# Attention output turned feature-major by 32x32 block transposes on VectorE and by its trip through HBM, in place of 64 transposes on TensorE

## The chip, the cores and the metric

The kernel runs on one core of one Trainium2 chip. The metric is the device time of that core in microseconds (us). Three runs of the kernel before gave 1374.78, 1375.06 and 1375.9 us; the median, 1375.06 us, is the time before.

## The reference

One layer of a hybrid encoder block, in float32, on x of 1024 tokens by 1024 features. Cut to what matters here:

```python
h = rmsnorm(x, norm_mix)
q, k, v, r, lr_f, lr_b, u, g_a, g_b = split(h @ w_in)
# gated linear attention, 4 heads (keys 128 wide, values 256 wide), forward and backward
o = gla(q, k, v, decay_fwd) + flip(gla(flip q, flip k, flip v, decay_bwd))
o = o * rsqrt(mean(o * o, axis=-1) + EPS)        # per head and token
o = o.reshape(tokens, 1024) * gla_norm           # one gain per feature
o = o * silu(r)                                  # the output gate
y_a = o @ w_branch_gla
...
merged = sigmoid(g_a) * y_a + sigmoid(g_b) * y_b # y_b: the pooling branch, from u
x = x + merged @ w_out
...                                              # feed-forward layer, last norm
```

The place of the change is between `o` and `y_a`: the four heads' normalized outputs are multiplied by the gain and by silu(r), and become an operand of the product with `w_branch_gla`.

## The kernel before

**Numbers.** Every large product runs as three products on TensorE: each f32 operand is split in a high part (a cast on ScalarE) and a low part (a subtraction on VectorE or GpSimd), and `products` (line 273) adds high x high, high x low and low x high into one PSUM bank. `mm3` (line 275) is such a triple, 512 columns wide as a rule, and calls `pump` behind it.

**Order of the work.** The program's order is written out by hand, and each engine runs its instructions in that order. A generator for the attention of a head yields after each part, with the cost of the part in units of one 512-wide triple. `pump` counts the triples down and lets the next thing into the program when its time has come: first what `soon(delay, ...)` put off, then a split of weights that were loaded, then the jobs that run beside, then the next part of the attention. So attention's small steps lie between the triples of the projections.

**Memory.** SBUF holds 39 slots of 128 x 1024 f32, given out in turn; four buffers for raw weights, six each for their high and low parts; five small temporaries (`t2`). PSUM has three banks for the large products and five for all else (`ps_g`).

**Loads and writes.** All of them are issued on SyncE's queue, in program order: an issue that waits holds up all issues behind it. Weights are loaded by `load` (line 208) one step ahead of use, cast to the high part on ScalarE (line 200), and the low part is made on GpSimd (line 201). Writes to HBM are not issued where the data is made: `later` notes them, and `flush` (line 563) issues all that are noted.

**The attention of head h** (`attention`, from line 813) makes the decays, the keys, the chunk states and scores, and at its end, for each of eight token tiles, 128 tokens x 256 values of output, copied to one of two slots `o[half]` of 4 x 256 per partition (line 999). Tokens lie on the partitions, features along the row. `rms_scale` (line 1012) makes the norm's factors. `normalize` (line 1016) scales the eight tiles with one VectorE instruction each (line 1019). For heads 0 to 2 it then notes two writes to `o_out[h]`; it is called from the next head's attention, and the writes are issued some 3.5 units later. For head 3 it is called where the attention ends, and head 3's output stays in SBUF. That end falls inside the last triple of half 0 of column tile j = 3 of the loop below.

**The r loop** (lines 1212 to 1242) projects six of r's eight column tiles, j = 0 to 5, 128 features each. The result is feature-major: features on the partitions, tokens along the row, 512 of them in each of two halves. Each turn:

- at j = 2, 3 and 4 reads back the output of head 0, 1 and 2 (`load_o`, line 1033; tiles `ol`);
- takes the weights of j and issues the load and the splits of the next (`take`);
- at j = 4 loads the weights of the gate unit 0 (`fraw`, line 1085), which are the last two column tiles of r;
- for each half runs eight triples (`feature_major`), and after half 0 calls `flush` (line 1231);
- for j < 3 keeps r in SBUF (the attention isn't done yet); from j = 3 on gates one of the kept tiles and its own.

From j = 3 on, `feature_parts` (line 669) also runs beside: it reads eight sums of h back from HBM (`hs`, line 673), which ScalarE casts (`trh`, line 707) and VectorE subtracts from (`trl`, line 698), for products in Strassen's manner (seven products for eight blocks, from sums of blocks). The gate units' weights are combined in the same manner (`fs`, line 1093).

**The gate** (`gated`, line 1182) takes one feature tile of 128 and one half of 512 tokens: Silu of r on ScalarE (`sr`, line 1185); four transposes of 128 x 128 on TensorE into one PSUM bank `tp` (line 1188), since the attention's output is token-major and r is feature-major; then one VectorE instruction that multiplies the bank by the gain and by `sr` (line 1195). When a pair of tiles is whole for both halves, two writes of the gated output are noted and flushed 2 units later. The last two feature tiles are gated after the loop, when gate unit 0 is done. Eight tiles by two halves by four transposes are the 64 transposes.

Of the kernel before, what the change touches and what calls it, by code (L numbers as in the profile page):

```python
# [10 lines left out]
F32 = mybir.dt.float32  # L11
# [4 lines left out]
ALU = mybir.AluOpType  # L16

P = 128
# [3 lines left out]
NT = SEQ // P  # L22
HALF = 512
HEADS = 4
DK = 128
DV = 256
RANK = 16
CH = 128
SUB = 64
GROUPS = 4  # L30
WINDOWS = (2, 4, 8, 16)
PAD = 8
# [21 lines left out]
def kernel(  # L54
# [20 lines left out]
    nc = tc.nc  # L75
# [10 lines left out]
    ps_g = ctx.enter_context(tc.tile_pool(name="ps_g", bufs=8 - MM_BANKS, space=bass.MemoryType.PSUM))  # L86

    dram = ctx.enter_context(tc.tile_pool(name="dram", bufs=1, space=bass.MemoryType.DRAM))
# [4 lines left out]
    def name(s):  # L93
        count[0] += 1
        return f"{s}_{count[0]}"

    def slot(dtype=F32, shape=(2, HALF), s="slot"):
        return slots.tile([P, *shape], dtype, tag="slot", name=name(s))

    def t2(width=HALF, dtype=F32, s="t"):  # L100
        return tmp.tile([P, width], dtype, tag="t2", name=name(s), padded_shape=[P, HALF + 2 * PAD])
# [4 lines left out]
    def vec(width, s="v"):  # L106
        return small.tile([P, width], F32, tag="vec", name=name(s), bufs=12)

    def bank(pool, s="ps"):
        return pool.tile([P, HALF], F32, tag=pool.name, name=name(s))  # L110
# [5 lines left out]
    ident = const.tile([P, P], F32, tag="ident", name="ident")  # L116
# [8 lines left out]
    keep = const.tile([P, 4, P], U8, tag="keep", name="keep")  # L125
    carry = const.tile([P, HALF // SUB, SUB], BF16, tag="carry", name="carry")

# [5 lines left out]

    edge = const.tile([P, 2, GROUPS, PAD], F32, tag="edge", name="edge")
    nc.gpsimd.memset(edge[:, :, :, :], 1.0)
# [18 lines left out]
    def soon(delay, *steps):  # L154
        put_off.extend([delay, step] for step in steps)
# [146 lines left out]
    def rms_scale(ms, width, s):  # L302
        rs = vec(width, s)
        nc.vector.tensor_scalar(rs[:, :], ms, EPS, None, op0=ALU.add)
        nc.gpsimd.tensor_tensor(rs[:, :], rs[:, :], half_neg[:, :width], op=ALU.pow)
        return rs
# [132 lines left out]
    g_mix, g_ffn, g_gla, g_pool = (cols[:, 8 * i : 8 * i + 8] for i in range(4))  # L439
# [118 lines left out]
    def later(dst, src):  # L558
        deferred.append((dst, src))
# [174 lines left out]
    o_heads, unscaled = {}, []  # L734
# [78 lines left out]
    def attention(h):  # L813
# [28 lines left out]
        def decay(half, d):  # L842
# [3 lines left out]
            tot = vec(8, "tot")  # L846
            cs3 = cs.rearrange("p (n c) -> p n c", c=SUB)
            la3 = la.rearrange("p (n c) -> p n c", c=SUB)
            cy = carry.rearrange("p n c -> p (n c)")
            if d == 0:  # L850
                nc.vector.tensor_tensor_scan(cs[:, :], cy, la[:, :], 0.0, op0=ALU.mult, op1=ALU.add)
                nc.vector.tensor_copy(tot[:, :], cs3[:, :, SUB - 1])
            else:
# [4 lines left out]
                )  # L858
                nc.vector.tensor_tensor(tot[:, :], cs3[:, :, SUB - 1], la3[:, :, SUB - 1], op=ALU.add)
            first = cs.rearrange("p (n a c) -> p n a c", a=2, c=SUB)[:, :, 0, :]  # L860
            tot2 = tot.rearrange("p (n a) -> p n a", a=2)
# [62 lines left out]
        def scores(half):  # L924
            sc = [bank(ps_g, "sc") for _ in range(2)]
            for d in range(2):
                for i in range(4):
                    n = 4 * half + i
                    nc.tensor.matmul(
                        sc[d][:, i * CH : (i + 1) * CH], chunk_of(ke, n, d), chunk_of(qe, n, d),  # L930
                        start=True, stop=True,
                    )
            hi, lo = (t2(dtype=F32R, s="p")[:, :] for _ in range(2))
            nc.vector.copy_predicated(sc[1][:, :], keep.rearrange("p n c -> p (n c)"), sc[0][:, :])
            split_to(hi, lo, sc[1][:, :])
            return hi, lo
# [8 lines left out]
        q, k = qk_heads[h]  # L945
# [21 lines left out]
        for n in range(NT - 1, 0, -1):  # L967
            m = n - 1
# [9 lines left out]
        p = scores(0)  # L978
# [3 lines left out]
        o = [slot(shape=(4, DV), s="o") for _ in range(2)]  # L982
        ms = vec(NT, "oms")
        old = sf = None
        for n in range(NT):
            half, i = n // 4, n % 4
# [22 lines left out]
            if n == 3:  # L1009
                p = q_next  # L1010
            yield 1.02
        rs = rms_scale(ms[:, :], NT, "ors")
        if h == HEADS - 1:
            o_heads[h] = o

        def normalize():
            for n in range(NT):
                t = o[n // 4][:, n % 4, :]
                nc.vector.tensor_scalar(t, t, rs[:, n : n + 1], None, op0=ALU.mult)
            if h < HEADS - 1:  # L1020
                for half in range(2):
                    later(o_out[h][:, 4 * half : 4 * half + 4, :], o[half][:, :, :])

        unscaled.append(normalize)
        if h == HEADS - 1:
            unscaled.pop()()

    o_out = [dram.tile([P, NT, DV], F32, name=f"o_out{h}") for h in range(HEADS - 1)]

    def load_o(h):  # L1030
        o_heads[h] = [slot(shape=(4, DV), s="ol") for _ in range(2)]
        for half in range(2):
            nc.sync.dma_start(o_heads[h][half][:, :, :], o_out[h][:, 4 * half : 4 * half + 4, :])

    def sums_behind():
        prepare_beside(map(feature_sums, range(2)), 2)
# [21 lines left out]
    for h in range(HEADS):  # L1058
        if h:
            project_qk(h, h == 2)  # L1060
        else:
            first_qk()
            begin(attention(0))
        if h < HEADS - 1:
            begin(attention(h + 1))
        if h == 0:
            for ts in ((7,), (6,), (5, 4)):
                pair_products(ts)
            prepare_beside(map(branch_jobs, range(4)), 4.2)
        if h == 2:  # L1070
            value_weights.pop().products()
# [110 lines left out]
    def gated(j, half, src):  # L1182

        sr = t2(s="sr")
        nc.scalar.activation(sr[:, :], src, AF.Silu)
        tp = bank(ps_g, "tp")
        for i in range(4):
            nc.tensor.transpose(
                tp[:, i * P : (i + 1) * P],
                o_heads[j // 2][half][:, i, (j % 2) * P : (j % 2 + 1) * P], ident[:, :],  # L1190
            )
        if j // 2 not in oT:
            oT[j // 2] = [slot(s="o") for _ in range(2)], []
        tiles, there = oT[j // 2]
        nc.vector.scalar_tensor_tensor(
            tiles[half][:, j % 2, :], tp[:, :], g_gla[:, j : j + 1], sr[:, :], op0=ALU.mult, op1=ALU.mult
        )
        there.append((j, half))
        if len(there) == 4:
            c = j // 2 % 2  # L1200
            for half, t in enumerate(tiles):
                later(ob_out[j // 4, half][:, 2 * c : 2 * c + 2, :], t[:, :, :])
            soon(2, flush)

    def put_by():

        if raw_r:
            gated(*raw_r.pop(0))
# [3 lines left out]
    for j in range(KT - 2):  # L1212
        if 2 <= j <= 4:
            load_o(j - 2)
# [8 lines left out]
        for half in range(2):  # L1223
            if j >= BY and not sums_begun and (j > BY or not side):
                finish_side()
                finish_beside()
                prepare_beside([feature_parts()], 5)
                sums_begun = True
            ps = feature_major(w, hT, half)
            if half == 0:  # L1230
                flush()
            elif j == KT - 3:
                for _ in range(2):
                    gunits[1].load()
            if j < BY:
                nc.scalar.copy(whole_r[:, half, :], ps[:, :])
                raw_r.append((j, half, whole_r[:, half, :]))
            else:
                put_by()
                gated(j, half, ps[:, :])  # L1240
            if j == KT - 3 and half == 0:
                gates_ahead.step()
# [155 lines left out]

    p_out = dram.tile([GROUPS, 2, P, 2, HALF], F32, name="p_out")
    u_rows = [dram.tile([P, SEQ], F32, name=f"u_rows{g}") for g in range(GROUPS)]  # L1400

# [28 lines left out]
    def pooling():  # L1430

        for g in range(GROUPS):
            u = [t2(HALF + 2 * PAD, s="u") for _ in range(2)]
# [630 lines left out]
    for at, p in enumerate(OUT_ORDER):  # L2064
# [9 lines left out]
        for i in range(CLOSE if closing else n_of):  # L2074
            n = at * n_of + i
# [57 lines left out]
```

## Time and profile before

| what | value |
|---|---|
| median of three runs | 1375.06 us (1374.78 to 1375.9) |
| the profiled execution: span from its first to its last instruction | 1373.4 us |
| TensorE, matmuls | 1361.4 us busy, 99% |
| VectorE | 836.8 us, 61% |
| GpSimd | 752.1 us, 55% |
| ScalarE | 647.3 us, 47% |
| mean granted TensorE clock | 0.999 |
| read and written in HBM | 168.74 MB and 82.05 MB, 183 GB/s over the span |

The profile is of one execution. Times in it are microseconds, or nanoseconds where a row gives a mean for one instruction. PE is TensorE's matmuls and transposes, PEld its loading of weights (which runs beside the matmuls), DVE is VectorE, ACT ScalarE, POOL GpSimd, SP SyncE, which issues the transfers. `L1188` is line 1188 of the kernel. A row such as `o<-tp,cols,sr` names the tile that is written and the tiles that are read, without their numbers. A timeline row begins with the time from the span's start and the duration. A row of waits names an engine, the tile that the waiting instruction writes, and behind the arrow the instruction that released it, with the longest waits in us. Matmuls are pipelined: one of 512 columns lasts 0.39 us from its start to its end, and the next starts before it has ended.

In time, the four attentions lie before some 330 us, the gate's products run from 324.5 to 383.0 us, the last Silu of the r loop is at 353.6 us, and the branches, the merge and the feed-forward layer fill the rest.

### The profile page before, as it was taken

How to read it: one execution, taken by the hardware profiler on the slowest of the kernel's cores; microseconds unless marked ns; L12 is line 12 of the kernel's file. 1: busy time of each engine (PE TensorE's matmuls, PEld its weight loads, DVE VectorE, ACT ScalarE, POOL GpSimd, SP SyncE). 2: the span in 40 equal slices, each digit the busy share in tenths (PEclk: the TensorE clock that was granted, in tenths of full speed). 3: DMA queues.
4: the chain of work that ended last, by engine and by line, in shares of the span. 5: the costliest groups of instructions: out<-in, count | busy, mean ns of one | idle time of the engine just before them, and what ended most of it. 6: DMA issues, size and time to landing. Idle time of an engine off the chain costs nothing. (4 is left out here: it accounts for less than half of the span.)

```text
span 1373.4 us, 17879 instructions
## 1 busy us (share of the span) xinstructions
PE 1361.4 (99%) x6310; PEld 1132.9 (82%) x6310; DVE 836.8 (61%) x1034; ACT 647.3 (47%) x1177; POOL 752.1 (55%) x557
## 2 busy tenths in 40 slices
PE   9999999999999999999999999999999999999998
PEld 7888888888888888888888888888888888888886
DVE  6974556554735777678883955655566556343375
ACT  7365666755534445554346533333333334444253
POOL 3323723222597547667764376666676667455454
PEclk9999999999999999999999999999999999999999
DMA  6321523314778569995416355555544447985451
GB/s 227 113 87 52 181 90 92 95 60 123 245 236 278 186 198 308 373 386 216 150 71 241 112 174 176 176 176 177 176 145 137 146 136 266 384 301 187 169 215 77
DMA packets 167834, 251.97 MB, mean 183 GB/s; under 512 B 11160, under 2 KB 94144, under 8 KB 167744
## 3 DMA queue, kind: packets, MB, share of 16 engines
q1 hardware_dynamic: 167600, 250.57, 53.8%
q8 instruction: 49, 0.80, 0.2%
q14 instruction: 41, 0.34, 0.1%
q10 hardware_dynamic: 144, 0.26, 0.0%
HBM read 168.74 MB, written 82.05 MB: 183 GB/s over the span
## 5 line engine op out<-in xcount | busy, mean ns | idle before, releaser
L201 POOL TENSOR_TENSOR wl<-fs,wh 128x512 fp32r<-128x512 f32 x124 | 173.1, 1400 | 163.5 <-ACT wh L200 104.0
L273 PE MATMUL ps<-gh,wh 128*128 128x512 f32 x616 | 240.5, 390 | 0.0
L273 PE MATMUL ps<-gl,wh 128*128 128x512 f32 x616 | 239.8, 389 | 0.3 <-DVE gl L1691 0.3
L273 PE MATMUL ps<-gh,wl 128*128 128x512 f32 x616 | 239.7, 389 | 0.0
L201 POOL TENSOR_TENSOR wl<-fraw,wh 128x512 fp32r<-128x512 f32 x93 | 134.0, 1442 | 75.0 <-ACT wh L200 72.4
L201 POOL TENSOR_TENSOR ol<-gor,oh 128x1024 fp32r<-128x1024 f32 (+1 forms) x42 | 101.3, 2417 | 86.0 <-ACT oh L200 71.7
L273 PE MATMUL ps<-hh,wh 128*128 128x512 f32 x356 | 145.1, 408 | 0.7 <-ACT ga L1474 0.7
L273 PE MATMUL ps<-hh,wl 128*128 128x512 f32 x356 | 139.0, 390 | 0.0
L273 PE MATMUL ps<-hl,wh 128*128 128x512 f32 x356 | 138.8, 390 | 0.0
L273 PEld LDWEIGHTS ps<-gl,wh 128*128 128x128 f32 x616 | 115.7, 188 | 24.5 <-DVE gl L1691 0.7
L273 PEld LDWEIGHTS ps<-gh,wh 128*128 128x128 f32 x616 | 115.7, 188 | 24.1 <-ACT hb L1710 0.2
L273 PEld LDWEIGHTS ps<-gh,wl 128*128 128x128 f32 x616 | 115.7, 188 | 23.9
L273 PE MATMUL ps<-oh,oh 128*128 128x512 f32 x308 | 119.8, 389 | 0.0
L273 PE MATMUL ps<-ol,oh 128*128 128x512 f32 x308 | 119.8, 389 | 0.0
L273 PE MATMUL ps<-oh,ol 128*128 128x512 f32 x308 | 119.8, 389 | 0.0
L201 POOL TENSOR_TENSOR wl<-wraw,wh 128x512 fp32r<-128x512 f32 x56 | 92.3, 1679 | 44.7 <-ACT wh L200 44.6
L201 POOL TENSOR_TENSOR wl<-raw,wh 128x512 fp32r<-128x512 f32 x34 | 47.4, 1404 | 108.3 <-ACT wh L200 71.9
L201 DVE TENSOR_TENSOR ol<-wor,oh 128x1024 fp32r<-128x1024 f32 (+1 forms) x42 | 62.8, 1506 | 68.1 <-ACT oh L200 55.5
L200 ACT CAST wh<-fs 128x512 fp32r<-128x512 f32 x124 | 76.1, 615 | 29.5 <-DVE fs L1093 28.3
L273 PEld LDWEIGHTS ps<-hh,wl 128*128 128x128 f32 x356 | 66.8, 188 | 14.4
L273 PEld LDWEIGHTS ps<-hh,wh 128*128 128x128 f32 x356 | 67.0, 188 | 13.1 <-ACT ga L1474 1.1
L273 PEld LDWEIGHTS ps<-hl,wh 128*128 128x128 f32 x356 | 67.0, 188 | 12.0
(281 smaller groups left out, 3073.4 us busy)
## 6 DMA issues: line engine op xcount, KB each, us to landing
fraw<-in_w_ffn_in_dram SPq DMA_DIRECT2D x44, 512.0 KB, 6.1
gor<-g_out SPq DMA_DIRECT2D x35, 512.0 KB, 6.1
fraw<-in_w_in_dram SPq DMA_DIRECT2D x22, 512.0 KB, 6.5
g_out<-s SPq DMA_DIRECT2D x44, 256.0 KB, 2.3
wor<-t_out SPq DMA_DIRECT2D x20, 512.0 KB, 3.7
raw<-in_w_in_dram SPq DMA_DIRECT2D x36, 256.0 KB, 5.1
g_out<-g SPq DMA_DIRECT2D x33, 256.0 KB, 2.6
x<-in_x_dram SPq DMA_DIRECT2D x16, 512.0 KB, 5.6
```

Source lines behind the costliest of these rows:

```text
L200: nc.scalar.copy(hi, src)
L201: eng.tensor_tensor(lo, src, as_f32(hi), op=ALU.subtract)
L273: nc.tensor.matmul(ps, a[i], b[j], start=first and n == 0, stop=last and n == 2, skip_group_check=onto)
```

## The change

Three things are done differently.

First, the output of each head is partly turned before it is written. After the scaling (the same eight instructions per head, now half by half), one VectorE instruction per half transposes the slot in blocks of 32 x 32 into a new slot `turned`: the row of the block goes to the place along the row, and 32 neighbouring features land on 32 partitions. What a block transpose leaves undone, moving the blocks between partitions, is done by the write: `o_out[h]` is now laid out as 256 features by 512 tokens for each half, and four writes per half, one for each group of 32 partitions, put the blocks where they belong. Tokens of a feature lie in HBM in the order (i, n, b): partition group i, tile n, place b.

Second, head 3 makes the same trip through HBM. At the end of its attention, its writes are flushed 3 units later, or by an earlier flush, and read back 9 units later. All four heads are read by `load_o` with features on the partitions.

Third, `gated` issues no transposes and takes no bank for them. In place of one VectorE product of 128 x 512 from PSUM it issues four of 128 x 128 from SBUF, one for each i, because the tokens of the two operands are in a different order.

```diff
+SQ = 32
...
-        if h == HEADS - 1:
-            o_heads[h] = o
 
         def normalize():
-            for n in range(NT):
-                t = o[n // 4][:, n % 4, :]
-                nc.vector.tensor_scalar(t, t, rs[:, n : n + 1], None, op0=ALU.mult)
-            if h < HEADS - 1:
-                for half in range(2):
-                    later(o_out[h][:, 4 * half : 4 * half + 4, :], o[half][:, :, :])
+            for half in range(2):
+                for n in range(4):
+                    t = o[half][:, n, :]
+                    nc.vector.tensor_scalar(t, t, rs[:, 4 * half + n : 4 * half + n + 1], None, op0=ALU.mult)
+                turned = slot(shape=(DV // SQ, 4 * SQ), s="ot")
+                nc.vector.transpose(
+                    turned[:, :, :].rearrange("p k (n b) -> p n k b", b=SQ),
+                    o[half][:, :, :].rearrange("p n (k a) -> p n k a", a=SQ),
+                )
+                to = o_out[h][half].rearrange("(k a) (i m) -> i a k m", a=SQ, i=4)
+                for i in range(4):
+                    later(to[i], turned[i * SQ : (i + 1) * SQ, :, :])
 
         unscaled.append(normalize)
         if h == HEADS - 1:
             unscaled.pop()()
-
-    o_out = [dram.tile([P, NT, DV], F32, name=f"o_out{h}") for h in range(HEADS - 1)]
+            soon(3, flush)
+            soon(9, partial(load_o, h))
+
+    o_out = [dram.tile([2, DV, HALF], F32, name=f"o_out{h}") for h in range(HEADS)]
 
     def load_o(h):
-        o_heads[h] = [slot(shape=(4, DV), s="ol") for _ in range(2)]
+        o_heads[h] = [slot(s="ol") for _ in range(2)]
         for half in range(2):
-            nc.sync.dma_start(o_heads[h][half][:, :, :], o_out[h][:, 4 * half : 4 * half + 4, :])
+            nc.sync.dma_start(o_heads[h][half][:, :, :], o_out[h][half].rearrange("(j p) t -> p j t", p=P))
...
         sr = t2(s="sr")
         nc.scalar.activation(sr[:, :], src, AF.Silu)
-        tp = bank(ps_g, "tp")
-        for i in range(4):
-            nc.tensor.transpose(
-                tp[:, i * P : (i + 1) * P],
-                o_heads[j // 2][half][:, i, (j % 2) * P : (j % 2 + 1) * P], ident[:, :],
-            )
...
-        nc.vector.scalar_tensor_tensor(
-            tiles[half][:, j % 2, :], tp[:, :], g_gla[:, j : j + 1], sr[:, :], op0=ALU.mult, op1=ALU.mult
-        )
+
+        def every(t, i):
+            return t.rearrange("p (n i b) -> p i n b", n=4, b=SQ)[:, i]
+
+        turned = o_heads[j // 2][half][:, j % 2, :].rearrange("p (i n b) -> p i n b", i=4, b=SQ)
+        for i in range(4):
+            nc.vector.scalar_tensor_tensor(
+                every(tiles[half][:, j % 2, :], i), turned[:, i], g_gla[:, j : j + 1], every(sr[:, :], i),
+                op0=ALU.mult, op1=ALU.mult,
+            )
```

## The prediction

> **What bounds the kernel now.** I read the page first (busy shares, clock), then the waits of TensorE, then the chain that ended last.
>
> ```profile
> span 1373.4 us, 17879 instructions
> PE 1361.4 (99%) x6310; PEld 1132.9 (82%) x6310; DVE 836.8 (61%) x1034; ACT 647.3 (47%) x1177; POOL 752.1 (55%) x557
> PEclk9999999999999999999999999999999999999999
> PE warm L461 <- POOL ident masks.py:199: 1.4, 1, 1.4
> PE ps L273 <- POOL wl L201: 0.6, 2, 0.4
> 761.27 601.99 PE ps L273 x2654
> ```
>
> TensorE is busy for 1361.4 of 1373.4 us at a granted clock in the top tenth. Its longest wait is 1.4 us, and 602 us of the last chain are matmuls of one line back to back. So TensorE's own instruction stream sets the time: whatever is taken out of it is gained, and whatever makes it wait is lost in full, because nothing later waits for a fixed moment. The median of the three runs, 1375.06 us, is 1.7 us over the profiled span; I add and subtract on the span and put the difference on that median. About 0.2% (2.75 us) is what a measurement of this kernel can tell from no change.
>
> **What is removed: 64 transposes.** The first four rows are TensorE's timeline around one group of eight, the last two the groups by shape.
>
> ```profile
> 319.68 0.40 PE L273 MATMUL ps<-hh,wl 128*128 128x512 f32 x1
> 319.91 1.04 PE L1188 MATMUL tp<-ident,ol 128*128 128x128 f32 x8
> 320.70 0.47 PE L273 MATMUL ps<-hh,wh 128*128 128x512 f32 x1
> 321.02 0.39 PE L273 MATMUL ps<-hl,wh 128*128 128x512 f32 x1
> L1188 PE MATMUL tp<-ident,ol 128*128 128x128 f32 x48 | 6.2, 273 | 0.0
> L1188 PE MATMUL tp<-ident,o 128*128 128x128 f32 x16 | 2.4, 272 | 0.0
> ```
>
> One transpose lasts 273 ns, but they overlap. From 319.68 to 321.02 are 1.34 us; without the eight, two steps of 0.23 us would lie there (319.68 to 319.91 is one). So eight cost 0.88 us, one 0.11 us, and 64 cost 7.0 us (the busy times, 6.2 + 2.4 us, count the overlap with the next matmul and are an upper bound). With no new wait the kernel would take 1375.06 - 7.0 = 1368.1 us. Six groups of eight leave between 319.9 and 352.5 us (5.3 us), four of four later (1.8 us).
>
> **What VectorE gets.** The norm's scaling is regrouped but costs the same. New are two block transposes per head, and four products of 128x128 in place of one of 128x512.
>
> ```profile
> 322.36 2.19 DVE L1019 TENSOR_SCALAR o<-o,ors 128x256 f32<-128x256 f32 x8 [1.75 <-POOL ors L305]
> L713 DVE TENSOR_TENSOR hs<-hs,hs x8: 1224/1226/2195, 50.0 to 68.6; 128x1024 f32<-128x1024 f32 x8
> L1195 DVE SCALAR_TENSOR_TENSOR o<-tp,cols,sr x16: 740/748/751, 324.5 to 383.0; 128x512 f32<-128x512 f32 x16
> L881 DVE TENSOR_TENSOR ke<-z,k 128x512 f32<-128x512 f32 x16 | 10.9, 682 | 3.1 <-ACT z L872 3.1
> L862 DVE TENSOR_TENSOR z<-z,tot 128x256 f32<-128x256 f32 x16 | 6.9, 432 | 0.5
> ```
>
> No block transpose is in this trace. [...] The small product, by the step from 256 to 512 elements (432 to 682 ns), costs about 0.3 us, so four cost 1.2 us against 0.75. VectorE then has some 10 us + 7 us more, in heads 0 to 2 in idle time before the next decay, in the r loop beside matmuls. None of it is on TensorE's path by itself.
>
> **What SyncE's queue gets, and who stands behind it.** This carries the forecast. A head's two writes become eight of a quarter size each, and head 3, which stayed in SBUF, now makes the trip too: normalize (line 1016) runs when attention(3) ends, inside the last product of j = 3, half 0, and the flush at line 1231 issues its eight writes at once, before the delayed one. The queue is in order and runs far ahead:
>
> ```profile
> 287.34 0.94 SPq L208 DMA_DIRECT2D raw<-in_w_in_dram  x2
> 296.21 0.34 SPq L673 DMA_DIRECT2D hs<-f_out  x1
> 310.60 0.81 SPq L1033 DMA_DIRECT2D ol<-o_out  x2
> 311.50 0.94 SPq L208 DMA_DIRECT2D raw<-in_w_in_dram  x2
> 312.53 3.81 SPq L1085 DMA_DIRECT2D fraw<-in_w_in_dram  x2
> 317.14 26.02 SPq L673 DMA_DIRECT2D hs<-f_out  x4
> ```
>
> In program order the eight writes stand right behind the first row (weights for j = 4). All the others, down to the second load of hs, stand behind the writes, which wait for VectorE: scaling from 322.36, 2.19 us, two transposes 2.4 us, done at 327.0. The first four writes go out between; the last four, at about 0.35 us each, end at 328.4. So loads that were issued at 296 to 319 us go out from 328.4 on: 17 us later for raw. Their slack is less than that, and I take the two places where it ends.
>
> ```profile
> o_out<-o SPq DMA_DIRECT2D x6, 512.0 KB, 2.8
> ol<-o_out SPq DMA_DIRECT2D x6, 512.0 KB, 4.0
> raw<-in_w_in_dram SPq DMA_DIRECT2D x36, 256.0 KB, 5.1
> hs<-f_out SPq DMA_DIRECT2D x8, 512.0 KB, 5.1
> 312.00:322.00 10.00, 10.00 (x60) 8.86 (x59) 3.04 (x8) 7.17 (x20) 3.87 (x3) 1.00 1.07 309
> 322.00:330.00 8.00, 8.00 (x41) 6.67 (x40) 4.92 (x12) 4.46 (x8) 2.61 (x3) 1.00 0.18 65
> 326.97 1.13 ACT L200 CAST wh<-raw 128x512 fp32r<-128x512 f32 x2
> 333.34 1.04 ACT L707 CAST trh<-hs 128x1024 fp32r<-128x1024 f32 x1
> 353.59 0.58 ACT L1185 ACTIVATE sr<-ps 128x512 f32<-128x512 f32 x1
> 354.75 6.95 POOL L201 TENSOR_TENSOR wl<-fs,wh 128x512 fp32r<-128x512 f32 x4 [4.35 <-ACT wh L200]
> 339.80 0.47 PE L273 MATMUL ps<-hh,wh 128*128 128x512 f32 x1
> 358.56 0.39 PE L273 MATMUL ps<-trh,wl 128*128 128x512 f32 x1
> ```
>
> First place: the weights of j = 5 (raw, cast at 326.97, first used at 339.80; their low half in the third matmul, 340.3). Four groups of transposes earlier, TensorE asks for that low half at 336.7. The raw load now has 1.5 MB of other loads ahead (hs, two of ol). At the 309 GB/s of 312 to 322 us (last column of its row) and about 3.4 us of fixed time (5.1 us to landing less 1.7 us of data), it lands at 336 to 338, plus 0.6 us cast and 1.3 us on GpSimd: 338 to 340. A wait of 1.5 to 3.5 us.
>
> Second place: product p = 6 of the first gate run, whose low weights are used at 358.56, in the new kernel at 353.3 without waits. ScalarE is in order, and its cast of those weights stands behind sr of j = 5 and behind the casts of hs number 4 and 5. Those loads need slots that the difference of hs number 2 frees, and number 2 was cast at 333.34. Call L the landing of number 2. Ahead of it from 328.4 stand 4.7 MB: hs, ol, raw, fraw, head 3's two reads and itself, 15 us at 309 GB/s; with the fixed time L = 347 (345 to 349). From L: cast 1.0, two sr 1.1, four products on VectorE 0.8, difference 1.2, load 4.0 to 5.1, the next load 1.2 behind it, its cast 1.0, two sr 1.1, weight cast 0.6, GpSimd 1.3: 13.3 to 14.4 us. So the weights are ready at 347 + 13.9 = 360.9, and TensorE has by then waited 7.6 us in all (5 to 10), the first place included.
>
> What is late after that: the weights of p = 5, 3 and 7 follow on GpSimd at 1.7 us each, while a product takes 2.7 us; they hold.
>
> [...]
>
> **Heads 0 to 2.** The writes there are delayed by 2.4 us of transposes and about 1.2 us of issues, so what follows in the queue goes out some 3.5 us later. Only after head 0 is there no slack:
>
> ```profile
> 135.43 2.41 SPq L563 DMA_DIRECT2D o_out<-o  x2
> 137.94 9.22 SPq L752 DMA_DIRECT2D raw<-in_w_in_dram  x5
> 155.17 1.30 POOL L713 TENSOR_TENSOR wsum<-wsum 128x512 f32<-128x512 f32 x1 [3.88 <-DMA wsum<-in_w_branch_gla_dram]
> ```
>
> GpSimd waits 3.88 us for a load that stands behind the raw loads and then works without a gap up to the wl for which TensorE already waits (0.4 us, above). If the raw loads move, that wait grows by 0 to 1.7 us. Several of the five wait for buffers anyway (9.22 us for five issues), so I take 0.5.
>
> **The sum.** -7.0 + 7.6 + 0.5 = +1.1 us: 1376.2 us. With the bounds of the two waits, -7.0 + 5 + 0 = -2.0 to -7.0 + 10 + 1.7 = +4.7.
>
> **Rivals.**
>
> Faster: the covers hold. If the transfers run faster than 309 GB/s, or the casts of hs do not stand in the way of the weights, waits of 0 to 4 us are left: 1368 to 1372 us. For it: from 322 to 330 us only 65 GB/s moved (a row above), so the transfers have the DMA engines to themselves; against it: the queue order follows from the code, and 17 us of delay are more than the 13 us from the cast to the use of raw.
>
> Slower: the block transpose runs at half rate, 2.4 us. Then the last write of head 3 leaves at 330.8, L moves to 349.4, the waits come to 10 us and more, and with head 0's at its upper end the time is 1379 to 1381. It decides from about 1.9 us for one transpose (waits of 9 us). For it: no row shows this instruction; against it: no VectorE row of 1024 f32 that ran undisturbed takes over 1.3 us.
>
> [...]
>
> **How the numbers follow.** The forecast's case has a chance of 0.5; of it 0.37 lies within 0.2%, 0.13 above. The covers hold: 0.25, of it 0.22 faster by over 0.2%. Half-rate transposes: 0.13, all but 0.02 above. The clock: 0.12, half of it above. That makes 0.22 faster, 0.48 the same, 0.30 slower. The range goes from 1370.5 (half of the first rival) to 1381 (the end of the slow one).
>
> **What would show it.** Right: no line with tp; TensorE waits for wl of raw at about 337 and for wl of fs at about 355, together 5 to 10 us; the loads of ol, raw and fraw for j = 4 and 5 issued at 329 or later, behind the writes of head 3; ScalarE idle for a DMA of raw from about 327; block transposes of about 1.2 us. Wrong: those loads still issued near 311, or no wait of TensorE over 1 us between 330 and 365 us (then it is 1368), or a clock digit below 9 near 360 us.

## The result and the profile after

Four runs of the changed kernel gave 1383.79 to 1385.80 us, median 1384.61, beside a median of 1374.92 us before: a ratio of 1.007 (95% interval 1.0055 to 1.0084). The kernel became 9.7 us slower, where 1.1 us (range -4.6 to +5.9) was forecast. The head of the page and the waits of TensorE in the changed kernel (us in all, times, longest):

```profile
span 1382.9 us, 17832 instructions
PEclk9999999999899999999999999999999999999999
PE ps L274 <- ACT ga L1483: 9.1, 2, 8.4
PE ps L274 <- ACT wh L201: 3.3, 1, 3.3
PE ps L274 <- POOL wl L202: 0.9, 2, 0.7
```

Before, no wait of TensorE in this part was over 1 us; now there is one of 3.3 us, with 0.7 us close behind it, and one of 8.4 us, and one digit of the clock fell below 9. The queue of SyncE (issue time, duration, count):

```profile
325.20 4.17 SPq L564 DMA_DIRECT2D o_out<-ot  x8
329.50 0.39 SPq L674 DMA_DIRECT2D hs<-f_out  x1
329.99 1.30 SPq L1041 DMA_DIRECT2D ol<-o_out  x2
331.40 1.78 SPq L209 DMA_DIRECT2D raw<-in_w_in_dram  x2
333.28 5.05 SPq L1093 DMA_DIRECT2D fraw<-in_w_in_dram  x2
```

Head 3's eight writes stand first, the loads behind them: raw goes out at 331.4 instead of 311.5 us. TensorE's timeline at the two waits (the bracket is the idle time before an instruction and what ended it):

```profile
336.40 0.39 PE L274 MATMUL ps<-hh,wl 128*128 128x512 f32 x1
340.04 0.50 PE L274 MATMUL ps<-hh,wh 128*128 128x512 f32 x1 [3.25 <-ACT wh L201]
340.38 0.39 PE L274 MATMUL ps<-hl,wh 128*128 128x512 f32 x1
341.45 0.80 PE L274 MATMUL ps<-hh,wl 128*128 128x512 f32 x1 [0.68 <-POOL wl L202]
342.04 0.63 PE L274 MATMUL ps<-hh,wh 128*128 128x512 f32 x1
...
345.14 0.40 PE L274 MATMUL ps<-hh,wl 128*128 128x512 f32 x1
```

```profile
358.78 0.39 PE L274 MATMUL ps<-hh,wl 128*128 128x512 f32 x1
367.59 0.79 PE L274 MATMUL ps<-trh,wh 128*128 128x512 f32 x1 [8.42 <-ACT ga L1483]
368.18 0.63 PE L274 MATMUL ps<-trl,wh 128*128 128x512 f32 x1
...
372.28 0.40 PE L274 MATMUL ps<-trh,wl 128*128 128x512 f32 x1
```

Read the start times: a step is 0.23 us at the high clock and 0.43 where the granted clock is halved (0.50 of full speed from 342 to 344 us and from 366 to 372 us, 1.00 from 345 to 346). In the first stretch the steps exceed 0.23 us by 3.4 + 0.1 + 0.8 = 4.4 us of waiting and 1.6 us of low clock (341.45 to 345.14). In the second they exceed it by 8.6 us of waiting and 2.2 us of low clock (367.59 to 372.28). Together 16.8 us, less 7.0 us for the transposes: 9.8, and the span grew by 9.5.

The second wait is not ended by weights, but by `ga`, the copy of product p = 1 out of its PSUM bank (`Gates.run`), into which p = 6 then adds. ScalarE and VectorE ahead of it:

```profile
359.05 1.04 ACT L708 CAST trh<-hs 128x1024 fp32r<-128x1024 f32 x1 [2.67 <-DMA hs<-f_out]
360.00 0.62 ACT L1193 ACTIVATE sr<-r 128x512 f32<-128x512 f32 x1
360.54 0.58 ACT L1193 ACTIVATE sr<-ps 128x512 f32<-128x512 f32 x1
361.01 1.12 ACT L201 CAST wh<-fs 128x512 fp32r<-128x512 f32 x2
366.43 0.62 ACT L201 CAST wh<-fs 128x512 fp32r<-128x512 f32 x1 [4.29 <-DVE fs L1101]
366.96 0.58 ACT L1483 COPY ga<-ps 128x512 f32<-128x512 f32 x1
```

```profile
361.60 4.20 DVE L1203 SCALAR_TENSOR_TENSOR o<-ol,cols,sr 128x128 f32<-128x128 f32 x8
365.72 0.68 DVE L1101 TENSOR_TENSOR fs<-fraw,fs 128x512 f32<-128x512 f32 x1
```

The copy stands behind the cast of p = 3's weights in ScalarE's order; the cast waits for VectorE's sum `fs`; the sum stands behind eight products of two gates; and those wait for the Silus, which stand behind a cast of hs that waits for its load. The same chain before the change, and TensorE at p = 6:

```profile
352.11 1.05 ACT L707 CAST trh<-hs 128x1024 fp32r<-128x1024 f32 x1 [2.13 <-DMA hs<-f_out]
...
356.64 0.62 ACT L200 CAST wh<-fs 128x512 fp32r<-128x512 f32 x1 [1.44 <-DVE fs L1093]
357.16 0.58 ACT L1474 COPY ga<-ps 128x512 f32<-128x512 f32 x1
```

```profile
353.86 1.41 DVE L1195 SCALAR_TENSOR_TENSOR o<-tp,cols,sr 128x512 f32<-128x512 f32 x2
355.19 1.42 DVE L1093 TENSOR_TENSOR fs<-fraw,fs 128x512 f32<-128x512 f32 x1
```

```profile
357.88 0.39 PE L273 MATMUL ps<-hh,wl 128*128 128x512 f32 x1
358.10 0.39 PE L273 MATMUL ps<-trh,wh 128*128 128x512 f32 x1
```

The copy ended at 357.74 us and p = 6 began at 358.10: there was 0.4 us of slack, and no view of waits shows it, because nobody waited. From the start of that cast of hs to the start of the copy, the chain takes 5.1 us before the change (352.11 to 357.16) and 7.9 us after it (359.05 to 366.96).

### The profile page after: what moved, and what is told of

The parts are those of the page before. It is cut to its first block, busy times and chain, and to the rows that moved or that the text cites. A ratio compares the mean times of both kernels' runs of the same rounds, so it can differ in the third digit from the quotient of the medians.

```text
span 1382.9 us, 17832 instructions
## 1 busy us (share of the span) xinstructions
PE 1359.5 (98%) x6246; PEld 1129.2 (82%) x6246; DVE 857.0 (62%) x1090; ACT 647.1 (47%) x1177; POOL 754.1 (55%) x557
## 5 line engine op out<-in xcount | busy, mean ns | idle before, releaser
L274 PE MATMUL ps<-trh,wh 128*128 128x512 f32 x176 | 69.6, 395 | 8.4 <-ACT ga L1483 8.4
```

The source lines that it names most:

```text
L274: nc.tensor.matmul(ps, a[i], b[j], start=first and n == 0, stop=last and n == 2, skip_group_check=onto)
```

## The experiments

My theory of the change, called **queue theory** in the expectations: head 3's writes block the queue, both waits come from that, and without the block the 7 us are gained. Its rivals: **VectorE** is made late by the new products; and, from the second round on, the **chain**: the casts, gates and copies on ScalarE and VectorE set when p = 6 can start, whatever TensorE saves. "p = 6" is the start of that product in the profiled run; the wait is TensorE's before it.

| run | median us | ratio to before (95%) | span | p = 6 | wait |
|---|---|---|---|---|---|
| before (1374.9 to 1375.2 in each batch) | 1374.92 | | 1373.4 | 358.1 | 0 |
| the change | 1384.61 | 1.0070 (1.0055 to 1.0084) | 1382.9 | 367.6 | 8.4 |
| e1 writes later | 1377.78 | 1.0023 (1.0014 to 1.0032) | 1376.1 | 360.3 | 7.5 |
| e2 raw first | 1378.05 | 1.0020 (1.0011 to 1.0029) | 1377.1 | 360.7 | 7.2 |
| e3 transposes back | 1386.70 | 1.0086 (1.0072 to 1.0100) | 1384.4 | 367.1 | 5.8 |
| e4 before, no transposes | 1371.94 | 0.9978 (0.9969 to 0.9988) | 1370.3 | 356.7 | 3.5 |
| e5 change, filled | 1382.77 | 1.0058 (1.0044 to 1.0072) | 1380.5 | 367.3 | 1.3 |
| e6 before, blocked | 1382.48 | 1.0051 (1.0036 to 1.0067) | 1382.0 | 366.8 | 0 |
| e21 heads 0 to 2 | 1377.39 | 1.0012 (1.0003 to 1.0021) | 1376.1 | 358.1 | 4.9 |

The profiled executions are apart already ahead of the place of the change. The last matmul ahead of the first transposes begins at 319.68 us before, at 320.07 in the change, 319.71 in e1, 320.47 in e2, 320.18 in e4, 321.38 in e6, 318.86 in e7, 320.15 in e8, 321.00 in e9, 319.84 in e16 and 320.11 in e21. Where the text compares two times of p = 6 "from the same start", this difference is taken off.

**Head 3's writes later (e1).**

```diff
-            soon(3, flush)
-            soon(9, partial(load_o, h))
...
         if j == 5:
             gates_ahead.step()
+            load_o(HEADS - 1)
...
-            if half == 0:
+            if half == 0 and j != BY:
                 flush()
```

> The changed kernel, but head 3's eight writes are issued half a column tile later (at the flush of j = 4), behind the loads of j = 4 (weights of j = 5, fraw) and two loads of hs, and its two reads come at j = 5. Queue theory: the loads go out near 311 to 319 us as before the change, neither of the two long waits of TensorE is left, and the 64 transposes are gained: 1375 - 7 = 1368 us (1367 to 1370). VectorE theory (the four products from SBUF and the block transposes make VectorE late): the first wait, for a load, goes, but the second still ends near 367 us: 1380 us or more.

Measured: 1377.78 us. The loads went out near 311 to 319 us, the first wait went, and 6.8 us with it. The second stayed:

```profile
352.36 0.39 PE L274 MATMUL ps<-hh,wl 128*128 128x512 f32 x1
360.30 0.79 PE L274 MATMUL ps<-trh,wh 128*128 128x512 f32 x1 [7.55 <-ACT ga L1482]
360.89 0.63 PE L274 MATMUL ps<-trl,wh 128*128 128x512 f32 x1
```

TensorE reached the end of p = 2 at 352.36 instead of 357.88 us: the 48 transposes ahead of it are worth 5.5 us, as priced (5.3). It then stood for 7.5 us. Half of the queue theory fell.

**The transposes back (e3)**, in the changed kernel, read by nobody:

```diff
+        tp = bank(ps_g, "tp")
+        for i in range(4):
+            nc.tensor.transpose(
+                tp[:, i * P : (i + 1) * P], o_heads[j // 2][half][:, j % 2, i * P : (i + 1) * P], ident[:, :],
+            )
```

> The changed kernel with the 64 transposes of TensorE put back, of the tiles ol as they lie, into a bank that nobody reads. Queue theory: the second wait ends at a time that the queue of loads sets (367.5 us of the span), so the 48 transposes ahead of it (5.3 us) are swallowed by shorter waits, the 16 behind it cost 1.8 us, and shorter waits can spare some of the clock's loss: 1383 to 1387 us, against 1384.6. Plain sum (waits and work add up): 1384.6 + 7 = 1391.6 us.

Measured: 1386.70 us, 2.1 more than the change, where 7 us of work were added. p = 6 began at 367.1 as against 367.6. What TensorE does ahead of p = 6 does not count there.

**No transposes in the kernel before (e4).**

```diff
-        tp = bank(ps_g, "tp")
-        for i in range(4):
-            nc.tensor.transpose(
...
         nc.vector.scalar_tensor_tensor(
-            tiles[half][:, j % 2, :], tp[:, :], g_gla[:, j : j + 1], sr[:, :], op0=ALU.mult, op1=ALU.mult
+            tiles[half][:, j % 2, :], o_heads[j // 2][half][:, 2 * (j % 2) : 2 * (j % 2) + 2, :].rearrange("p n c -> p (n c)"), g_gla[:, j : j + 1], sr[:, :], op0=ALU.mult, op1=ALU.mult
```

> The kernel before with its 64 transposes left out; the product of the gate reads the attention's output as it lies, token-major, so the turning is left out and nothing takes its place. At 0.11 us for a transpose, as the steps between matmuls give: 1375 - 7.0 = 1368 us. At their busy time, 8.6 us: 1366.4. If that stretch is held by casts or loads as soon as TensorE is ahead: 1370 to 1374.

Measured: 1371.94 us, only 3.1 us less. The profile shows where 3.9 us of the 7.0 went:

```profile
352.83 0.39 PE L273 MATMUL ps<-hh,wl 128*128 128x512 f32 x1
356.68 0.50 PE L273 MATMUL ps<-trh,wh 128*128 128x512 f32 x1 [3.47 <-ACT ga L1468]
357.02 0.39 PE L273 MATMUL ps<-trl,wh 128*128 128x512 f32 x1
```

p = 6 came 1.4 us earlier (1.9 from the same start), and the 16 transposes behind it gave 1.8 us: 3.2. But the edit does more than leave the transposes out: the product now reads two tiles of SBUF in place of a bank and one tile. On VectorE the products of two gates and the sum behind them took longer than before (1.41 and 1.42 us there):

```profile
351.39 2.44 DVE L1189 SCALAR_TENSOR_TENSOR o<-ol,cols,sr 128x512 f32<-128x512 f32 x2
353.75 1.74 DVE L1093 TENSOR_TENSOR fs<-fraw,fs 128x512 f32<-128x512 f32 x1
```

From the cast of hs (348.91 us) to the copy (356.05) the chain took 7.1 us in place of 5.1. At its old length the copy would have come 2 us earlier (an estimate), so more than half of the wait is the longer chain's, and only the rest is what the kernel before had no room for. No run leaves out the transposes and keeps the products as they were.

**TensorE kept busy in the waits (e5)**, in the changed kernel; `fill(n)` issues n matmuls of 128x512 into a bank that nobody reads:

```diff
+            if j == 5 and half == 0:
+                fill(12)
...
+            if (self.kind, p) == ("r", 6):
+                fill(34)
```

> The changed kernel with matmuls that nobody reads put ahead of the two matmuls that wait: 12 (2.7 us) ahead of j = 5 and 34 (7.8 us) ahead of p = 6, so that TensorE works through most of both waits. Idle theory (the lower granted clock after each wait comes from TensorE standing idle): the clock stays high, the 3.4 us of slow matmuls go: 1381 us. Rival (the clock falls for another reason, or the slow matmuls are part of the wait for operands): 1384.6 or more.

Measured: 1382.77 us, mean clock 0.999 against 0.994, no slow step. So in this kernel the low clock comes from standing idle. But only 1.8 us were gained (by the medians; the two intervals overlap), about the second stretch's 2.2: p = 6 began at 367.3, as without the filling, so what was saved in the first stretch was waited away there.

**The block alone (e6)**, in the kernel before; `spare` is a tile in HBM that nobody reads:

```diff
             unscaled.pop()()
+            for half in range(2):
+                turned = slot(shape=(DV // SQ, 4 * SQ), s="ot")
+                nc.vector.transpose(
+                    turned[:, :, :].rearrange("p k (n b) -> p n k b", b=SQ),
+                    o[half][:, :, :].rearrange("p n (k a) -> p n k a", a=SQ),
+                )
+                to = spare[half].rearrange("(k a) (i m) -> i a k m", a=SQ, i=4)
+                for i in range(4):
+                    later(to[i], turned[i * SQ : (i + 1) * SQ, :, :])
```

> The kernel before, in which head 3's output, beside staying in SBUF, is also block-transposed and written to HBM by eight writes at the place of the change; nobody reads them. TensorE keeps its 64 transposes and the gate its products from PSUM. Chain theory (the time is set by when the copy of p = 1 out of its bank, behind casts on ScalarE, lets p = 6 start; the blocked queue makes that chain late): p = 6 starts between 361.3 and 364.7 us (367.5 less 2.8 us for shorter products, less up to 3.4 for the missing reads) against 358.1: 1378 to 1382 us, and up to 2 us more for the clock. VectorE theory (only the new products are at fault): 1375 to 1376 us.

Measured: 1382.48 us, 7.5 more than before. The block, with its two block transposes, costs about what e1 gave back. The place was another than I expected: TensorE waited 4.4 us, until 339.3 us, for head 2's reads, which its own transposes need, and p = 6 came at 366.8 without a wait. The chain, whose products still read the bank, took 5.1 us from the cast of hs (360.74) to the copy (365.80), as before.

**Copy ahead of the cast (e7)** and **weights ahead of the gates (e8)**, both on e1. The first block is in both, the second in e8 alone, which also drops the two steps behind the loop:

```diff
+            if (n, at) == (0, 0):
+                zs[of].run(p)
+                gates_ahead.step()
+                continue
...
+                if (j, half) == (KT - 3, 1):
+                    for _ in range(AHEAD - 2):
+                        gates_ahead.step()
                 put_by()
```

> The first experiment (head 3's writes later), with the cast of the weights of p = 3 put behind p = 1 in the program, so that the copy of p = 1's bank no longer stands behind it on ScalarE. Chain theory: the wait at p = 6 ends with the weights of p = 6 (cast at 355.2 us, low part at 356.6) and not at 360.3 us: 3.7 us less, and up to 2 us of the clock's loss: 1372 to 1374 us. If something else holds p = 6: 1377.8 us as before.

> The kernel with the copy ahead, and with the weights of p = 6 and p = 5 combined and cast ahead of the last gates of the r loop instead of behind them. Chain theory: TensorE reaches p = 6 at 352.4 us with nothing left to wait for, and the 64 transposes are gained in full: 1368 to 1371 us. If the sums of h (hs) hold p = 6 or p = 5: 1372 us or more.

Measured: e7 1374.60 us, 3.2 us less than e1 and just over the forecast; p = 6 began at 355.4, from the same start 4.0 us earlier than in e1: the cast did hold the copy. e8 1374.70 us, p = 6 at 356.7, from the same start no earlier than in e7: missed by 4 us. In both the copy then stood behind the two Silus and the cast of hs ahead of them (ScalarE was idle for its load until 351.8 and 353.1 us); moving the weights changed the order of the casts, not that one.

**One product (e9)**, on e1:

```diff
-        for i in range(4):
-            nc.vector.scalar_tensor_tensor(
-                every(tiles[half][:, j % 2, :], i), turned[:, i], g_gla[:, j : j + 1], every(sr[:, :], i),
+        nc.vector.scalar_tensor_tensor(
+            tiles[half][:, j % 2, :], o_heads[j // 2][half][:, j % 2, :], g_gla[:, j : j + 1], sr[:, :],
...
```

> The first experiment (head 3's writes later), with the gate's product as one instruction of 128x512 in place of four of 128x128; it takes the tokens in the order in which they lie, so the restoring of their order is left out. Chain theory: the two gates ahead of the weights of p = 3 take 1.5 to 3.2 us in place of 4.2 on VectorE, p = 6 starts 1.0 to 2.7 us earlier: 1375 to 1377 us. If the four products do not lie on the chain: 1377.8 us.

Measured: 1376.47 us, 1.3 less (the two intervals overlap). p = 6 began at 359.9, 0.4 us earlier than in e1, or 1.7 from the same start. The two gates' products took 1.4 us instead of 4.2, but the sum behind them, which also reads two tiles of SBUF, now took 1.75 in place of 0.68:

```profile
355.58 1.41 DVE L1197 SCALAR_TENSOR_TENSOR o<-ol,cols,sr 128x512 f32<-128x512 f32 x2 [2.35 <-ACT sr L1191]
356.92 1.75 DVE L1099 TENSOR_TENSOR fs<-fraw,fs 128x512 f32<-128x512 f32 x1
```

From the cast of hs to the copy the chain took 5.2 us (353.98 to 359.22) in place of 7.0 in e1 (352.65 to 359.66). So the products lie on it, and part of what they gave was lost in the next instruction.

**The chain cut (e11, b11, e12)**: the weights of p = 5 and 6 cast after half 0 of j = 5, p = 3's step behind p = 1, and the order of the products:

```diff
-    R_RUN = 1, 2, 6, 5, 3, 7, 4
+    R_RUN = 1, 2, 5, 6, 3, 7, 4
```

> The first experiment (head 3's writes later), and the chain to p = 6 cut: the weights of p = 5 and p = 6 are combined and cast after half 0 of j = 5, ahead of the last gates; the weights of p = 3 come behind p = 1; and product p = 5, which takes a fresh bank, runs ahead of p = 6, so that the copy of p = 1's bank has 2.7 us more. Chain theory: all three waits of that stretch go (p = 6, the clock, 0.8 us before p = 3): 1367 to 1370 us. If TensorE's release of slots in j = 5 and the loads of hs behind it hold p = 5 as well: 1372 to 1375 us.

> The kernel before with the same three moves alone, its 64 transposes kept. Chain theory: before the change the chain ended 0.4 us ahead of TensorE, so only the 0.8 us before p = 3 is to be had: 1374 to 1375 us. If the moves bring more than that by themselves (1373 us or less), the gain of the run beside it is not the transposes'.

> The kernel before without its transposes (the turning left out), with the same three moves. Chain theory: the 64 transposes bring their whole 7.0 us, which brought 3.1 us without the moves, and 0.8 us before p = 3: 1367 to 1368.5 us. If the price of a transpose is smaller than 0.11 us: 1371 to 1372 us as without the moves.

Measured: 1375.11, 1374.09 and 1371.32 us. The wait before p = 5 and 6 went (p = 5 at 353.2 us in e11), and TensorE waited 5.0 us (e12: 2.9) before p = 3 instead, for the copy of p = 5, which now stood behind the cast for p = 7. In the kernel before, the same moves brought 1.1 us (ratio 0.9992, 0.9983 to 1.0001). The wait moved. e11's time lies at the edge of the second answer, but p = 5 was not held, as that answer has it. e12 missed: its time is the second answer's, but that one's reason, a smaller price of a transpose, is not what the trace shows. (Its executions lie between 1369.53 and 1372.85 us, and the profiled one is the fastest.)

**Raw first (e2)**: as e1, but the flush and head 3's reads at the start of j = 4, around the loads of fraw:

```diff
         if j == 4:
+            flush()
             for _ in range(2):
                 gunits[0].load()
+            load_o(HEADS - 1)
```

> The changed kernel with head 3's eight writes one step later in the queue: behind the weights of j = 5 and head 2's reads, but still ahead of fraw and of the second load of hs. Chain theory: the wait for the weights of j = 5 goes, with its part of the clock's loss, but the end of the wait at p = 6 moves only by what is no longer ahead of hs (0 to 3.4 us), so that most of the first wait is swallowed: 1380 to 1384 us. Plain sum: the first wait and its clock (5.8 us) are saved in full: 1378.8 us.

Measured: 1378.05 us, the plain sum and not my expectation. fraw and hs went out at 329.9 and 333.7 us, behind the writes, and p = 6 began at 360.7, as in e1. So writes ahead of fraw and hs alone do not move p = 6. In the change the loads of hs go out 7 us later still (340.7), and TensorE is itself late by its first wait; which of the two moves p = 6 from 360.3 to 367.6, no run separates.

**Reads late (e16), with the chain cut (e17), and the controls (b17, e18).** e16 is e1 with `load_o(HEADS - 1)` behind the loop. The cut is that of e11, with p = 7's step behind p = 5:

```diff
+            if not n:
+                zs[of].run(p)
+                for _ in range((1, 0, 1, 1, 2, 1)[at]):
+                    gates_ahead.step()
```

> The first experiment (head 3's writes later), with head 3's two reads moved from the start of j = 5 behind the r loop, so that their two slots and 1 MB come after the chain to p = 6. Slot theory (head 3's extra tiles push the sums of h onto slots that TensorE frees only in j = 5, which starts the chain to p = 6 two loads late): p = 6 starts 3 us or more earlier than at 360.3 us: 1372.5 to 1374.5 us. If the reads do not matter and only the order on ScalarE and VectorE does: 1377.8 us, or worse, where they come too late for the last gates.

> The run beside this one (head 3's writes and reads later), and the chain cut: weights of p = 5 and 6 ahead of the last gates, p = 5 ahead of p = 6, and each copy of a bank ahead of the cast of weights that stood before it: p = 3's behind p = 1, p = 7's behind p = 5. Chain theory: no wait over 1 us is left in that stretch, 1375 - 7 - 0.8 + (0 to 2) = 1367 to 1370 us. If a wait only moves to another place once more: 1372 us or more.

> The kernel before with the same moves of weights and products alone, its transposes kept. Chain theory: the 0.8 us before p = 3 is all that is to be had: 1374 to 1375 us. If 1372 us or less, the moves and not the transposes make the gain of the run beside it.

> The kernel before without its transposes (the turning left out), with the same moves. Chain theory: with no copy behind a late cast, the 64 transposes bring 7.0 us and the moves 0.8: 1367 to 1368.5 us. If other waits end there: 1370 us or more.

Measured: 1376.47, 1373.96, 1374.13 and 1373.23 us. e16 missed: p = 6 came 0.2 us earlier, not 3. b17 came as expected. In e17 and e18 the chain theory's first answer missed and the second held: TensorE waited 4.3 and 3.9 us before p = 3, for p = 5's copy, which now stood behind a cast of hs that had waited 3.8 us (e18: 3.1) for the gates' products on VectorE. With the same moves, the kernels with and without the change are level.

**Heads 0 to 2 alone (e21)**: head 3 stays in SBUF and is turned on TensorE as before.

```diff
-            soon(3, flush)
-            soon(9, partial(load_o, h))
+            o_heads[h] = o
...
+        if j // 2 == HEADS - 1:
+            tp = bank(ps_g, "tp")
...
```

> The change for heads 0 to 2 alone: 48 of the 64 transposes go, all of them ahead of p = 6; head 3 stays in SBUF and is turned by TensorE as before, so there is no block of the queue and there are no further slots. Queue theory alone: 1375 - 5.3 = 1370 us, for nothing is left to wait for. Chain theory: TensorE reaches p = 6 some 5.3 us earlier and waits there for the copy of p = 1's bank, which comes at its old time (358 us) or, with the four products, up to 2 us later: 1374 to 1378 us, and the gain of the transposes is swallowed.

Measured: 1377.39 us. No block, 48 transposes gone, and still 2.2 us slower than before:

```profile
352.75 0.39 PE L274 MATMUL ps<-hh,wl 128*128 128x512 f32 x1
358.07 0.79 PE L274 MATMUL ps<-trh,wh 128*128 128x512 f32 x1 [4.93 <-ACT ga L1495]
358.66 0.63 PE L274 MATMUL ps<-trl,wh 128*128 128x512 f32 x1
```

```profile
352.07 4.21 DVE L1215 SCALAR_TENSOR_TENSOR o<-ol,cols,sr 128x128 f32<-128x128 f32 x8
```

TensorE came 5.1 us earlier, p = 6 began when it did before (358.07 against 358.10), and the low clock behind the wait, eleven steps of 0.43 us and one of 0.59, cost 2.6 us; the profiled span is 2.7 us longer. The chain's start moved forward by 2 us (the cast of hs at 350.06 in place of 352.11); its products took 4.2 us in place of 1.4, which gave that back.

**The clock again (e19)**, on e17:

```diff
+            if (self.kind, p) == ("r", 3):
+                fill(17)
             product(self.unit, p, ps, right)
```

> The kernel with head 3's writes and reads later and the chain cut (1373.96 us), with 17 matmuls that nobody reads (3.9 us) ahead of p = 3, where TensorE waits 4.5 us. Idle theory: the clock stays high, and the slow matmuls after that wait (0.4 us and five times 0.2 us) go: 1372.5 us, about 2 us less than both kernels. If nothing but the wait counts: 1374 us.

Measured: 1372.62 us, ratio 0.9981 (0.9972 to 0.9990). This is the one version with the change that beats the kernel before clear of noise, by 2.6 us. It is 1.5 us below that kernel with the same moves (b17), but there the intervals overlap. TensorE works on through the wait, and no slow step is left:

```profile
359.23 4.01 PE L1189 MATMUL fill<-hh 128*128 128x512 f32 x17
363.72 0.50 PE L274 MATMUL ps<-hh,wh 128*128 128x512 f32 x1 [0.48 <-ACT ga L1490]
364.06 0.40 PE L274 MATMUL ps<-hl,wh 128*128 128x512 f32 x1
```

## Why the prediction was wrong

In the terms of its sum, -7.0 + 7.6 + 0.5: the transposes gave about what was priced; the waits came to 13.0 us (4.4 + 8.6) in place of 7.6; and the low clock cost 3.8 us (1.6 + 2.2), which the sum puts at nothing. The step that failed worst is the path to the second wait.

- **"With no new wait the kernel would take 1368.1 us" and, of VectorE's work, "None of it is on TensorE's path by itself": the first steps that failed.** The price of a transpose was right (5.5 us for 48 in e1). But the chain of casts, gates and copies ended only 0.4 us before TensorE came to p = 6, and the new products lie on that chain: from the cast of hs to the copy it takes 5.1 us in the kernel before and in e6, whose products read the bank, and 7.0 in e1, 7.4 in e21 and 7.9 in the change, whose four products a gate read SBUF. "Whatever is taken out of it is gained" holds only as far as the slack of the next chain. e4 gained 3.1 us and not 7.0, some half of the loss by the longer chain that its own edit brought.
- **The queue, right.** The eight writes stood where forecast, the loads went out from 329.5 on (forecast 328.4), and hs number 2 was cast at 347.8 (forecast 347). Putting the writes later gave back 6.6 to 6.8 us (e2 and e1), and the block put into the kernel before cost 7.5 (e6).
- **First place, right in kind, too small.** Forecast 1.5 to 3.5 us at 336.7; measured 4.4 us of waiting from 336.4. The casts of raw, which waited for its loads, began at 339.4 and 340.2, where raw was to land at 336 to 338. fraw's megabyte, issued right behind it, I had not counted; whether that is the reason was not tried.
- **Second place: the step that failed worst.** I let the wait end with the weights of p = 6, at 360.9. Their casts came at 361.0, and the low half was ready at 363.1, so the sum to there held within some 2 us. But the wait ended at 367.5, with the copy of p = 1's bank, which my chain did not have: it goes on over the products of two gates, the sum fs, the cast for p = 3 and the copy. And I put the whole wait down to the queue; e1 and e21 show one of 7.5 and 4.9 us there without the block.
- **The products, "about 0.3 us" each: half right.** Alone one takes 0.34 us (in the sum for the second place four of them stand at 0.8 us, where 0.3 each makes 1.2). But where GpSimd works at the same time, one takes up to 1.44, and two gates 4.2 us against 1.4: the rows of the groups show it, and GpSimd's row beside the two gates of 361.60 us.

```profile
L1203 DVE SCALAR_TENSOR_TENSOR o<-ol,cols,sr x64: 309/345/1439, 327.4 to 395.3; 128x128 f32<-128x128 f32 x64
L1021 DVE STREAM_TRANSPOSE ot<-o x8: 1245/1246/1248, 135.5 to 326.2; 128x1024 f32<-128x1024 f32 x8
361.70 2.64 POOL L202 TENSOR_TENSOR wl<-fs,wh 128x512 fp32r<-128x512 f32 x2 [5.61 <-ACT wh L201]
```

  (Shortest, median and longest in ns.) Two of these eight products took 1.35 us each, and each of the two ended 0.15 us after the GpSimd instruction beside it (363.21 after 363.06 us, 364.48 after 364.33). Of all 64, nine took 1.0 us or more, and a GpSimd instruction ran beside each of the nine; none without one beside it took over 0.36 us. Before, the product read PSUM and one tile of SBUF and took 740 to 751 ns, GpSimd or not.
- **The clock, at 0.12 among the chances, came true twice**, at 1.6 and 2.2 us, the first time after waits of 3.3 and 0.7 us, the second after one of 8.4. The profile before has no wait over 1.4 us and no clock digit below 9, so the 0.12 was the author's estimate. The prediction names a clock digit below 9 near 360 us as a sign that it is wrong, and there is one.
- **Block transpose and the writes, right:** 1.25 us each (forecast 1.2), so the half-rate rival is out. No row of the kernel before shows a block transpose: the 1.2 us behind the forecast's two at 2.4 us and VectorE's 10 us was the author's estimate. Head 3's eight writes, of 32 partitions each, were issued in 4.2 us, the writes of all heads landed 2.0 to 2.7 us after their issue, and the loads behind head 3's waited for the issues (hs went out at 329.5 us, behind the last of them at 328.9).
- **Heads 0 to 2, right as far as it can be seen:** forecast 0.5 us. The last matmul ahead of the transposes' place comes 0.4 us later than before (320.07 against 319.68), but profiles with and without the change differ there by as much (319.71 in e1, 320.18 in e4).

Left open is why the chain starts later in e1 (p = 6 at 360.3) than in e21 (358.1). In e1 the cast of hs ahead of the last Silus came at 352.65, in e21 at 350.06; head 3's further tiles in the slots would explain it, but e16, which moved two of the four, changed 0.2 us. It is argued, not shown.

## What to carry to other kernels

Before counting work taken from the busiest engine as a gain, find what it will wait for next, and by how much that is early now: a view of waits does not show a slack of 0.4 us, but two timelines side by side do. The chain that ends in a wait includes the bank or buffer that must come free, and whatever stands ahead of that copy in its engine's order, not only the operands. Where an operand moves from PSUM to SBUF, look at what its reader takes beside the other engines: here a product of 128x128 from SBUF took 0.34 us alone and up to 1.44 us beside GpSimd, where one of 128x512 from PSUM had taken 0.74 to 0.75 us either way. And a write that waits for fresh data does not belong ahead of loads on an in-order queue: putting head 3's writes later gave back 6.8 us (e1).

## What the runs showed of the hardware

A wait of 3.47 us (e4, profiled execution, mean clock 0.999) was followed by one step of 0.34 us and then by steps of 0.23 to 0.24; one of 3.53 us (e8, mean clock 0.996) by fourteen slow steps, the first of 0.59 us and the others of 0.43:

```profile
352.79 0.39 PE L274 MATMUL ps<-hh,wl 128*128 128x512 f32 x1
356.71 0.80 PE L274 MATMUL ps<-trh,wh 128*128 128x512 f32 x1 [3.53 <-ACT ga L1485]
357.30 0.63 PE L274 MATMUL ps<-trl,wh 128*128 128x512 f32 x1
...
362.85 0.41 PE L274 MATMUL ps<-trh,wl 128*128 128x512 f32 x1
```

The slow steps lasted 3.7 us after the first wait of the change, 4.7 after the second, and 6.1 us here. In the change the trace has the granted clock at one half for 3.41 us at the first wait (341.35 to 344.76) and for 10.24 us at the second (361.82 to 372.06). Filler matmuls in the waits were worth 1.3 us (e19 against e17) and 1.8 us (e5 against the change), by medians whose intervals overlap.
